# A Conformer stage re-divided between the engines: fewer weight blocks in its opening, the convolution's taps on ScalarE and VectorE alone, side products and last sums moved in TensorE's queue

## The chip, the cores and the metric

The kernel runs on one core of a Trainium2 chip. The metric is the device time of one execution in microseconds (us). Besides the time there is one execution taken with the hardware profiler; its trace lists every instruction of the five engines with start, duration and what ended the idle time before it. Engines are named as the profile does: PE is TensorE's matrix products and PEld its weight loads, DVE is VectorE, ACT is ScalarE, POOL is GpSimd, SP is the queue from which nearly all weight transfers are issued.

## What is computed

Two layers for 256 positions of width 2048. Layer 0 mixes tokens with a Conformer convolution module, layer 1 with a Mamba-2 mixer; each is followed by a squared-ReLU MLP. Shifts, scales and gates of every sub-layer come from a vector `c` by the product with `w_mod`. The change lies in layer 0's mixer:

```python
def conformer_conv(u, w_pw1, b_pw1, w_dw, b_dw, ln_g, ln_b, w_pw2, b_pw2):
    v = u @ w_pw1 + b_pw1                  # 2048 -> 4096
    a, gt = jnp.split(v, 2, axis=-1)
    v = a * jax.nn.sigmoid(gt)             # "GLU"
    v = causal_dwconv(v, w_dw, b_dw)       # 31 taps, per channel
    v = jax.nn.silu(layernorm(v, ln_g, ln_b))
    return v @ w_pw2 + b_pw2

mod = (sc @ w_mod[i] + b_mod[i])[:, None, :]         # sc = silu(c), 6 * 2048 values a layer
sh1, sc1, g1, sh2, sc2, g2 = jnp.split(mod, 6, axis=-1)
h = h + g1 * mix
h = h + g2 * sq_relu_mlp(rmsnorm(h) * (1 + sc2) + sh2, w1, w2)
```

## The kernel before

Activations lie with channels on partitions: 16 channel tiles of 128 channels by 256 positions. Weights come as tiles of 128x2048 f32, 1 MB each, through one SP queue that keeps the order of the program (`stream`). The buffers `w32` (three) hold weight tiles; `wm` (two) and `hid` (four) hold tiles of `w_mod`.

**The opening.** `native(list(range(FIRST)), glu)` works on the first FIRST blocks of `pw1` at once. A block is 512 of the 4096 output columns, that is two channel tiles with their gates. For each of four groups g of the inner dimension `vectors` first makes the modulated input `u[g]` from eight `w_mod` tiles (VectorE's `gemv`, line 255), then each block multiplies its weight tile with it on TensorE (line 583, 16 products of 128x128 by 128x256 a tile). The fourth group goes in halves, each after four of its eight `w_mod` tiles. With FIRST = 4 the fourth block has banks of the pool `ms` and its weight tiles lie in `hid` buffers.

**The convolution stage.** `glu` gates two channel tiles of a block (line 507 on ScalarE, line 508 on VectorE) into one of twelve padded buffers `vpad`. `conv(ct)` then makes 31 taps for a channel tile: 20 products on ScalarE (line 518, 128x256 each, four side by side in a tile), of which two sums of four-wide tiles run on GpSimd (lines 527 and 529) and one on VectorE (528); the other 11 taps are multiply-adds on VectorE (532); lines 534, 535 and 537 fold the four columns. Line 544 takes off the mean of the first tile (`st["m0"]`, from the product of line 541), line 547 squares for the variance. Between three convs each, one more block of `pw1` runs on TensorE.

**The moments.** Sums over channels are taken on TensorE: `moments(g)` adds four tiles and their squares into one `ms` bank (line 558). After the fourth call ScalarE copies the bank (625), TensorE spreads it over the partitions (627), and VectorE and ScalarE make mean and variance (629 to 637), normalise (643 to 648), apply SiLU (649) and split each value for the next product (414 and 415).

**Side products.** Other `w_mod` vectors are made meanwhile, one tile for each `pump`. Those in PE_GROUPS (24 tiles) run on TensorE: line 244 adds four tiles into a row of sums in an `ms` bank, ScalarE copies it (249), four small products turn it into columns (251), ScalarE copies these (253). All others run on VectorE (255, 128x2048 each). The number of tiles is set by RATE_PW1 (in the blocks of the convolution stage), BETWEEN (after the last conv), RATE_PW2 (in `pw2`) and RATE_OPEN (in the opening of the MLP); `need` makes at once what a stage can't start without.

**Order.** A scheduler fixes the order of instructions on each engine ahead of the run; `high_priority` lets a part go first, `issue_after(x)` holds a part behind instruction x. At run time every engine takes its instructions in this order.

The times below carry the line numbers of this text of the kernel:

## Time and profile before

| | us |
|---|---|
| three runs | 2697.23, 2691.67, 2695.97 (median 2695.97) |
| the profiled execution, its own time | 2696.91 |
| span of its instructions | 2695.1 |
| opening, first product to the first gate | 43.0 to 145.7 |
| convolution stage, first gate to the end of the last square | 145.7 to 371.9 |
| last sums and normalisation, to the first products of `pw2` | 371.9 to 402.8 |
| `pw2`, to its last product | 402.8 to 502.4 |
| opening of the MLP, as far as the fourth group's first product | 502.4 to 571.5 |
| the rest (MLP, Mamba, second MLP) | 571.5 to 2695.1 |

A row of the timeline reads: start, duration of the merged piece, engine, line, operation, written tile <- read tiles, shapes, xcount, and in brackets the idle time of the engine just before with what ended it. A product of f32 operands leaves two records in the trace, so x32 is 16 products. A row of the windows gives, for a stretch of time, the busy time of each engine with its count, then TensorE's granted clock (1.00 is full), the busy share of the DMA engines and what they moved. A row of groups ends in busy time, mean ns of one | idle time before them with its releasers. Instructions overlap a little, so the time of one in a row of equals is read from start to start.

### The profile page before, as it was taken

How to read it: one execution, taken by the hardware profiler on the slowest of the kernel's cores; microseconds unless marked ns; L12 is line 12 of the kernel's file. 1: busy time of each engine (PE TensorE's matmuls, PEld its weight loads, DVE VectorE, ACT ScalarE, POOL GpSimd, SP SyncE). 2: the span in 40 equal slices, each digit the busy share in tenths (PEclk: the TensorE clock that was granted, in tenths of full speed). 3: DMA queues.
4: the chain of work that ended last, by engine and by line, in shares of the span. 5: the costliest groups of instructions: out<-in, count | busy, mean ns of one | idle time of the engine just before them, and what ended most of it. 6: DMA issues, size and time to landing. Idle time of an engine off the chain costs nothing.

```text
span 2695.1 us, 37026 instructions
## 1 busy us (share of the span) xinstructions
PE 2540.8 (94%) x14561; PEld 2194.8 (81%) x14561; DVE 2021.8 (75%) x2679; ACT 1345.7 (50%) x2112; POOL 202.4 (8%) x210
## 2 busy tenths in 40 slices
PE   5977759989999999999999999999998999999998
PEld 3865529988888888888888888888897888888886
DVE  6489857898888888888878777888866555565565
ACT  2067554444443443445868666754444344443443
POOL 1033310000000000000100000000000101101000
PEclk9988869999999999999999999999999999999999
DMA  9944458888888888885655555578756555555553
GB/s 385 386 158 146 158 212 318 318 330 320 323 314 324 323 317 327 310 328 176 232 177 184 173 179 190 199 277 316 294 188 218 187 188 189 191 185 200 188 187 141
DMA packets 92593, 657.43 MB, mean 244 GB/s; under 512 B 10465, under 2 KB 10465, under 8 KB 14465
## 3 DMA queue, kind: packets, MB, share of 16 engines
q1 hardware_dynamic: 88274, 640.73, 64.9%
q0 software_dynamic: 3136, 10.59, 1.2%
q10 hardware_dynamic: 1008, 3.75, 0.4%
q8 instruction: 114, 1.87, 0.3%
q14 instruction: 61, 0.50, 0.1%
HBM read 652.83 MB, written 2.20 MB: 243 GB/s over the span
## 4 chain that ended last, share of the span: by engine, by line
PE 86%; DVE 9%; DMA 2%; ACT 1%; issue 1%; SPq 0%; POOL 0%; ACTq 0%; DVEq 0%
PE mm L312 66%; PE mm L364 4%; PE mm L363 4%; PE mm L362 4%; DVE taps L532 4%; PE mm L583 3%; DMA hid<-wmT 1%; DVE taps L534 1%; DVE wl L305 1%; DVE taps L528 1%; PE ms L1031 1%; PE ms L583 1%; DVE wm L255 1%; DMA wm<-wmT 0%; PE ms L244 0%
## 5 line engine op out<-in xcount | busy, mean ns | idle before, releaser
L312 PE MATMUL mm<-u,wh 128*128 128x512 f32 (+1 forms) x4544 | 1372.7, 365 | 13.6 <-ACT wh L304 6.5
L304 ACT CAST wh<-w 128x1024 fp32r<-128x1024 f32 x768 | 807.0, 1051 | 996.3 <-PE mm L312 766.0
L305 DVE TENSOR_TENSOR wl<-w,wh 128x1024 fp32r<-128x1024 f32 x768 | 941.2, 1229 | 455.9 <-ACT wh L304 453.1
L312 PE MATMUL mm<-u,wl 128*128 128x256 f32 x3840 | 1079.2, 283 | 0.7 <-DVE wl L305 0.6
L312 PEld LDWEIGHTS mm<-u,wh 128*128 128x128 f32 x4544 | 814.0, 191 | 157.2 <-ACT wh L304 7.6
L312 PEld LDWEIGHTS mm<-u,wl 128*128 128x128 f32 x3840 | 730.7, 191 | 8.8 <-DVE wl L305 4.7
L312 PE MATMUL mm<-hid,wh 128*128 128x512 f32 (+1 forms) x1344 | 448.3, 384 | 2.5 <-DVE acc L703 2.5
L312 PE MATMUL mm<-hid,wl 128*128 128x256 f32 x1280 | 358.1, 280 | 0.0
L255 DVE SCALAR_TENSOR_TENSOR wm<-wm,scb 128x2048 f32<-128x2048 f32 x133 | 303.9, 2285 | 6.6 <-DMA wm<-wmT 6.3
L312 PEld LDWEIGHTS mm<-hid,wh 128*128 128x128 f32 x1344 | 248.3, 188 | 54.5 <-DVE acc L703 2.8
L312 PEld LDWEIGHTS mm<-hid,wl 128*128 128x128 f32 x1280 | 242.5, 189 | 0.4 <-issue 0.2
L583 PE MATMUL mm<-u,w 128*128 128x256 f32 x896 | 207.6, 393 | 3.5 <-ACT u L500 3.5
L583 PEld LDWEIGHTS mm<-u,w 128*128 128x128 f32 x896 | 176.0, 198 | 38.2 <-issue 8.8
L364 PE MATMUL mm<-wh,hid 128*128 128x512 f32 x512 | 200.0, 391 | 0.0
L362 PE MATMUL mm<-wh,hid 128*128 128x512 f32 x512 | 199.9, 390 | 0.0
L363 PE MATMUL mm<-wl,hid 128*128 128x512 f32 x512 | 199.5, 390 | 0.0
L266 POOL TENSOR_TENSOR mod<-mod,par 128x4 f32<-128x4 f32 (+1 forms) x50 | 38.3, 765 | 1235.3 <-DVE wm L255 1075.6
L532 DVE SCALAR_TENSOR_TENSOR taps<-u,par,taps 128x256 f32<-128x256 f32 x176 | 117.9, 735 | 0.5
L255 DVE SCALAR_TENSOR_TENSOR hid<-hid,scb 128x2048 f32<-128x2048 f32 x35 | 80.0, 2288 | 45.0 <-DMA hid<-wmT 33.9
L364 PEld LDWEIGHTS mm<-wh,hid 128*128 128x128 f32 x512 | 96.1, 188 | 19.7
L362 PEld LDWEIGHTS mm<-wh,hid 128*128 128x128 f32 x512 | 96.2, 188 | 19.6
L363 PEld LDWEIGHTS mm<-wl,hid 128*128 128x128 f32 x512 | 96.1, 188 | 19.6
(211 smaller groups left out, 1766.2 us busy)
## 6 DMA issues: line engine op xcount, KB each, us to landing
w<-w SPq DMA_DIRECT2D x256, 1024.0 KB, 4.9
wm<-wmT SPq DMA_DIRECT2D x145, 1024.0 KB, 7.0
w<-win SPq DMA_DIRECT2D x80, 1024.0 KB, 4.9
hid<-wmT SPq DMA_DIRECT2D x47, 1024.0 KB, 8.4
w<-pw SPq DMA_DIRECT2D x44, 1024.0 KB, 5.1
w<-wout SPq DMA_DIRECT2D x32, 1024.0 KB, 6.7
acc<-ac_d POOLq DMA_DIRECT2D x16, 512.0 KB, 7.2
hid<-pw SPq DMA_DIRECT2D x4, 1024.0 KB, 7.2
```

The source lines that it names most:

```text
L255: nc.vector.scalar_tensor_tensor(out=w, in0=w, scalar=1.0, in1=self.scb, op0=ALU.mult, op1=ALU.mult, accum_out=m[:, i:i + 1])
L266: nc.gpsimd.tensor_tensor(out=m, in0=m, in1=self.col("b_mod", (layer * 6 + seg) * NT + 4 * kg + i0, n), op=ALU.add)
L304: nc.scalar.copy(out=wh, in_=w[:, s, :])
L305: nc.vector.tensor_tensor(out=wl, in0=w[:, s, :], in1=wh.bitcast(F32), op=ALU.subtract)
L312: mm = lambda out, lhsT, rhs, **kw: self.nc.tensor.matmul(out, lhsT=lhsT, rhs=rhs, skip_group_check=True, **kw)
L362: mm(banks[q], lhsT=hi, rhs=wh[:, k, :], start=g == 0 and t == 0, stop=False)
L363: mm(banks[q], lhsT=hi, rhs=wl[:, k, :], start=False, stop=False)
L364: mm(banks[q], lhsT=lo, rhs=wh[:, k, :], start=False, stop=g == 3 and t == 3)
L528: nc.vector.tensor_add(wide, wide, products(four("wl"), 12))
L532: nc.vector.scalar_tensor_tensor(out=o, in0=vp[:, k:k + T], scalar=self.col("w_dw", ct * TAPS + k), in1=o, op0=ALU.mult, op1=ALU.add)
L534: nc.vector.tensor_add(wide, wide, aside)
L583: nc.tensor.matmul(o, lhsT=w[:, t, j * P:(j + 1) * P], rhs=u[g][:, t, :], start=g == 0 and t == 0 and j < 2, stop=g == 3 and t == 3, skip_ ...
```

## The change

- **Three blocks open**: FIRST is 3, all in `w32` buffers and in `mm` banks; the fourth block runs as the first one of the convolution stage, five in all, behind conv 0.
- **Taps**: ScalarE makes 24 products, VectorE adds them in five four-wide sums and makes the other 7 taps. GpSimd makes none.
- **`close`** splits off from `conv` what needs the first tile's mean; for tile 0 it is called from a hook inside the block that follows.
- **Side products**: the row of sums lies in an `mm` bank. Its turning into columns is a method of its own, `columns`, called when the next row of sums has been copied. It and the moments are held behind the last product issued (`self.pe`). RATE_PW1 is 12 tiles over five blocks, BETWEEN is 8 ahead of the last moments and 4 behind the normalisation's instructions; `w_mod` tiles keep going round `wm` and two `hid` buffers.
- **Last moments**: `moments` serves tiles 0 to 11; its bank is copied and spread before the last convs. The sums of tiles 12 to 15 are added by products with `ones` straight into the bank that holds the spread sums.
- The square-root table is loaded behind the last gate, and the subtraction of the mean for the first group moves into the loop over its tiles.

```diff
-RATE_PW1 = spread(10, 16)
-BETWEEN = 10
+RATE_PW1 = spread(12, 20)
+BETWEEN = 8, 4
...
-FIRST = 4
+FIRST = 3
 OPEN = 3
-ACT_TAPS = 20
+ACT_TAPS = 24
...
             if i == 0:
-                self.row_sums = self.bank(self.ms, "ms")
+                self.row_sums = self.bank(self.mm, "mm")
...
             if i == 3:
                 row = self.t("t2", [P, 512], bufs=3)
                 nc.scalar.copy(out=row, in_=self.row_sums)
...
+                self.rows_left.append((row, m, layer, seg, g))
+                if len(self.rows_left) > 1:
+                    self.columns()
+            return
...
+    def columns(self):
+        nc = self.nc
+        row, m, layer, seg, g = self.rows_left.pop(0)
+        ps = self.bank(self.mm, "mm")
+        with self.tc.issue_after(self.pe):
+            for j in range(4):
+                nc.tensor.matmul(ps[:, j:j + 1], lhsT=row[:, j * P:(j + 1) * P], rhs=self.sel[:, :1],
+                                 start=j == 0, stop=True, skip_group_check=True)
+        nc.scalar.copy(out=m, in_=ps[:, :4])
+        self.mod_done(layer, seg, g)
...
             wide = products(four("wh"), 0)
-            pair = self.b("hid", [P, 8, T])
-            aside = products(pair[:, :4, :], 4)
-            nc.gpsimd.tensor_tensor(out=aside, in0=aside, in1=products(pair[:, 4:, :], 8), op=ALU.add)
-            nc.vector.tensor_add(wide, wide, products(four("wl"), 12))
-            nc.gpsimd.tensor_tensor(out=aside, in0=aside, in1=products(four("wl"), 16), op=ALU.add)
+            for k in range(4, ACT_TAPS, 4):
+                nc.vector.tensor_add(wide, wide, products(four("wl"), k))
             for k in range(ACT_TAPS, TAPS):
...
-            nc.vector.tensor_add(wide, wide, aside)
...
         native(list(range(FIRST)), glu)
-        self.rings = ("wm", "hid")
...
-        ct = 0
-        for b in range(FIRST, 8):
+        y = conv(0)
+        native([FIRST], glu, pump=pump, hook=lambda: close(0, y))
+        ct = 1
+        for b in range(FIRST + 1, 8):
             for _ in range(3):
-                conv(ct)
+                close(ct, conv(ct))
                 ct += 1
...
+            if b >= 6:
+                moments(b - 6)
             native([b], glu, pump=pump)
+        with self.tc.issue_after(st["gate"]):
+            nc.scalar.activation(out=self.t("rcol", [P, 2])[:, :1], in_=self.eps, func=AF.Sqrt)
+        self.pump(BETWEEN[0])
+        moments(2)
+        rows = self.t("t2", [P, 2 * T], bufs=3)
+        nc.scalar.copy(out=rows, in_=st["sums"])
+        ps = self.bank(self.mm, "mm")
+        with self.tc.issue_after(self.pe):
+            nc.tensor.matmul(ps, lhsT=self.sel, rhs=rows, start=True, stop=False, skip_group_check=True)
         while ct < NT:
-            conv(ct)
+            close(ct, conv(ct))
             ct += 1
-        moments(2)
-        self.pump(BETWEEN)
...
-            moments(3)
-            rows = self.t("t2", [P, 2 * T], bufs=3)
-            nc.scalar.copy(out=rows, in_=st["sums"])
-            ps = self.bank(self.mm, "mm")
-            nc.tensor.matmul(ps, lhsT=self.sel, rhs=rows, start=True, stop=True)
+            for i in range(12, NT):
+                for e in range(2):
+                    self.pe = nc.tensor.matmul(ps[:, e * T:(e + 1) * T], lhsT=self.ones, rhs=st["sq"][i][e], start=False,
+                                               stop=i == NT - 1, skip_group_check=True).ins
...
+        with self.tc.issue_after(self.pe):
+            self.pump(BETWEEN[1])
```

TensorE at the last moments, before: `lo` and `nrm` are the squares of the last tiles, `scol` marks a side product (its tile of `w_mod` in `hid` or `wm`), `bT` with `t` the turning into columns, and the last row is the spreading of the sums (line 627).

```order
L558 MATMUL ms_1254<-nrm_1821,ones 32x256
L244 MATMUL ms_1856<-wm_1861,scol 32x512 x4
L244 MATMUL ms_1856<-hid_1867,scol 32x512 x4
L244 MATMUL ms_1856<-wm_1873,scol 32x512 x4
L251 MATMUL ms_1856<-bT_114,t_259_1879 128x1 x4
L244 MATMUL ms_1890<-hid_1887,scol 32x512 x4
L244 MATMUL ms_1890<-wm_1895,scol 32x512 x4
L244 MATMUL ms_1890<-hid_1901,scol 32x512 x4
L244 MATMUL ms_1890<-wm_1907,scol 32x512 x4
L251 MATMUL ms_1890<-bT_114,t_265_1913 128x1 x4
L627 MATMUL mm_1933<-t_266_1931,bT_114 128x512
```

The same place in the changed kernel, where the spreading is line 634 and the direct sums are line 643:

```order
L571 MATMUL ms_1378<-sq_1582,ones 32x256
L634 MATMUL mm_1828<-t_281_1826,bT_114 128x512
L643 MATMUL mm_1828<-acc_203,ones 128x256
L643 MATMUL mm_1828<-lo_1629,ones 128x256
L643 MATMUL mm_1828<-acc_203,ones 128x256
L643 MATMUL mm_1828<-nrm_1875,ones 128x256
L643 MATMUL mm_1828<-acc_203,ones 128x256
L643 MATMUL mm_1828<-lo_1922,ones 128x256
L643 MATMUL mm_1828<-acc_203,ones 128x256
L643 MATMUL mm_1828<-nrm_1969,ones 128x256
L245 MATMUL mm_2057<-hid_2054,scol 32x512 x4
```

No side product stands between the last square and the sums any more: eight tiles stand ahead of the moments of tiles 8 to 11, four behind the last sum.

TensorE inside a block of the convolution stage, before (here `u_186` and `u_187` are the third and fourth group of the modulated input, `w` a weight tile):

```order
L244 MATMUL ms_857<-wm_1104,scol 32x512 x4
L583 MATMUL mm_1058<-u_186,w_168_1102 128x256 x2
L251 MATMUL ms_857<-bT_114,t_170_1110 128x1 x4
L583 MATMUL mm_1058<-u_186,w_168_1102 128x256 x6
L583 MATMUL mm_1059<-u_186,w_168_1102 128x256 x8
L244 MATMUL ms_1139<-hid_1136,scol 32x512 x4
L583 MATMUL mm_1058<-u_187,w_171_1134 128x256 x8
```

and in the changed kernel, in block 7:

```order
L245 MATMUL mm_1445<-hid_1685,scol 32x512 x4
L591 MATMUL mm_1639<-u_186,w_258_1683 128x256 x8
L591 MATMUL mm_1640<-u_186,w_258_1683 128x256 x8
L245 MATMUL mm_1445<-hid_1709,scol 32x512 x4
L269 MATMUL mm_1717<-bT_114,t_224_1415 128x1 x4
L591 MATMUL mm_1639<-u_187,w_260_1707 128x256 x8
L591 MATMUL mm_1640<-u_187,w_260_1707 128x256 x8
```

Before, the columns of a row of sums (`ms_857`) stood two products behind the last tile of the same row. Now they stand behind the last tile of the next row: `t_224` was copied from the bank `mm_1144`, whose last tile stands in block 6.

VectorE in the convolution stage, before, one channel tile (`hid` is GpSimd's sum):

```order
L528 TENSOR_TENSOR taps_926<-taps_926,taps_941 128x1024
L532 SCALAR_TENSOR_TENSOR taps_926<-u_185,par,taps_926 128x256 x11
L534 TENSOR_TENSOR taps_926<-taps_926,hid_931 128x1024
L535 TENSOR_TENSOR taps_926<-taps_926 128x512
L537 TENSOR_TENSOR taps_926<-taps_926 128x256
L544 TENSOR_TENSOR acc_200<-taps_926,ssum_739 128x256
```

and now, where the end of one tile (`taps_1090`) stands between the sums of the next (`taps_1237`):

```order
L539 TENSOR_TENSOR taps_1237<-taps_1237,taps_1242 128x1024
L544 TENSOR_TENSOR taps_1090<-taps_1090 128x512
L539 TENSOR_TENSOR taps_1237<-taps_1237,taps_1248 128x1024
L546 TENSOR_TENSOR taps_1090<-taps_1090 128x256
L539 TENSOR_TENSOR taps_1237<-taps_1237,taps_1254 128x1024
L558 TENSOR_TENSOR acc_201<-taps_1090,ssum_708 128x256
L539 TENSOR_TENSOR taps_1237<-taps_1237,taps_1260 128x1024
L539 TENSOR_TENSOR taps_1237<-taps_1237,taps_1266 128x1024
L542 SCALAR_TENSOR_TENSOR taps_1237<-u_186,par,taps_1237 128x256 x7
```

A channel tile has five wide sums in place of two, 7 taps in place of 11, and no operand from GpSimd.

More of the change, by code (lines that the diff above doesn't have):

```diff
@@ L164, in __init__ @@
         self.mod = {}
+        self.rows_left = []
         self.prologue()
@@ L634, in conformer @@
             nc.scalar.activation(out=var, in_=var, func=AF.Sqrt, bias=self.eps)
-            for t in range(4):
-                nc.vector.tensor_sub(dd[0][:, t, :], dd[0][:, t, :], mean)
             nc.vector.reciprocal(var, var)
```

66 lines of the change are left out of this document (32 added, 34 removed).

## The prediction

> **What bounds the kernel now.** The windows by stage come first, then the timeline of each engine where a stage waits.
>
> ```profile
> 43.00:145.70 102.70, 100.91 (x457) 88.15 (x458) 60.69 (x62) 7.94 (x16) 3.16 (x16) 1.00 0.86 351
> 145.70:371.90 226.20, 158.13 (x756) 121.61 (x759) 194.72 (x272) 149.48 (x371) 81.45 (x38) 0.83 0.42 154
> 371.90:402.80 30.90, 19.11 (x96) 5.83 (x88) 11.41 (x19) 13.60 (x25) 1.00 (x5) 0.67 0.75 306
> 402.80:502.40 99.60, 99.60 (x790) 94.80 (x791) 79.61 (x97) 45.96 (x70) 3.43 (x8) 0.97 0.87 330
> 502.40:571.50 69.10, 59.40 (x465) 58.35 (x463) 62.77 (x81) 28.95 (x40) 1.91 (x5) 0.91 0.80 314
> 571.50:2695.10 2123.60, 2093.35 (x11985) 1820.85 (x11985) 1587.76 (x2115) 1085.84 (x1564) 105.23 (x102) 0.99 0.66 238
> ```
>
> The last row, four fifths of the time, is TensorE's (2093 of 2124 us) and the change leaves it alone. In the opening TensorE is nearly full and the DMA at 351 GB/s. The convolution stage is VectorE's: 195 of 226 us, TensorE 158. In the last sums nothing is full. `pw2` is TensorE's again; in the opening of the MLP TensorE stands still for 9.7 us.
>
> Why VectorE needs 14 us for a channel tile is seen in its taps, once beside GpSimd's sums and once without:
>
> ```profile
> 349.28 8.50 DVE L532 SCALAR_TENSOR_TENSOR taps<-u,par,taps 128x256 f32<-128x256 f32 x11
> 309.33 4.45 DVE L532 SCALAR_TENSOR_TENSOR taps<-u,par,taps 128x256 f32<-128x256 f32 x11
> 357.88 1.23 DVE L534 TENSOR_TENSOR taps<-taps,hid 128x1024 f32<-128x1024 f32 x1
> 359.14 0.69 DVE L535 TENSOR_TENSOR taps<-taps 128x512 f32<-128x512 f32 x1
> 360.33 0.42 DVE L544 TENSOR_TENSOR acc<-taps,ssum 128x256 f32<-128x256 f32 x1
> L529 POOL TENSOR_TENSOR hid<-hid,taps 128x1024 f32<-128x1024 f32 x16 | 40.2, 2513 | 35.4 <-ACT taps L518 20.7 <-DVE taps L532 14.4
> ```
>
> Eleven taps cost 4.45 us alone (0.40 each) and 8.50 beside GpSimd, whose sum lasts 2.5 us: VectorE stands still meanwhile. TensorE waits too, for copies that stand far down in ScalarE's order:
>
> ```profile
> 171.39 1.19 PE L541 MATMUL mm<-taps,ones 128*128 128x256 f32 x2 [13.62 <-DVE taps L537]
> 237.78 1.84 PE L251 MATMUL ms<-bT,t 128*128 128x1 f32 x8 [16.02 <-ACT t L249]
> 265.60 14.08 PE L583 MATMUL mm<-u,w 128*128 128x256 f32 x64
> 279.61 1.06 PE L244 MATMUL ms<-hid,scol 128*32 128x512 f32 x8
> 309.35 1.86 PE L251 MATMUL ms<-bT,t 128*128 128x1 f32 x8 [18.23 <-ACT t L249]
> ```
>
> **The opening: -9.5 us.**
>
> ```profile
> 72.67 20.88 PE L583 MATMUL mm<-u,w 128*128 128x256 f32 x96
> 52.14 14.14 SPq L289 DMA_DIRECT2D w<-pw  x3
> 50.00:60.00 10.00, 10.00 (x48) 8.81 (x47) 9.33 (x9) 0.00 (x0) 0.00 (x0) 1.00 1.01 420
> 115.00:125.00 10.00, 10.00 (x48) 8.81 (x47) 3.09 (x4) 0.91 (x2) 0.31 (x2) 1.00 0.62 209
> 131.51 2.29 DVE L255 SCALAR_TENSOR_TENSOR hid<-hid,scb 128x2048 f32<-128x2048 f32 x1 [13.27 <-DMA hid<-wmT]
> 143.69 10.63 PE L583 MATMUL mm<-u,w 128*128 128x256 f32 x48 [1.79 <-ACT u L500]
> 145.72 0.47 ACT L507 ACTIVATE a<-mm,par 128x256 f32<-128x256 f32 x1 [0.39 <-PE mm L583]
> ```
>
> Three blocks need 20.9 us of TensorE a group, so four groups no longer fill it. What remains is the DMA: the last half waits for `w_mod` tiles (13.27 us). At 420 GB/s a tile takes 1.049 MB / 420 = 2.5 us. The first three weight tiles of group 1 are issued up to 66.3 (52.14 + 14.14) as TensorE frees the buffers, with three blocks as with four. From there 26 tiles land before; with about 2 us latency and the 5 us lost at 115 to 125 (209 of 420 GB/s) this gives 66.3 + 2 + 65 + 5 = 138.3. Now 23 tiles: 57.5, and of the loss I keep 3, since the third weight buffer still waits for TensorE: 128.8, 9.5 earlier. Bounds: 7.5 with the whole loss, 12.5 with none. [...]
>
> **The convolution stage: -33.5 us.** Each engine's share, from the first gate on.
>
> VectorE, a tile: five sums at 1.23, seven taps at 0.40, 0.69 + 2 x 0.42, and the gating 0.48: 11.0, for 16 tiles 176 us. No GpSimd stands in its way.
>
> ```profile
> 345.64 4.98 ACT L518 ACTIVATE taps<-u,par 128x256 f32<-128x256 f32 x12
> 367.77 1.71 ACT L669 ACTIVATE h<-h,gb 128x256 f32<-128x256 f32 x4 [0.90 <-POOL gb L666]
> 371.47 0.42 ACT L547 ACTIVATE nrm<-acc 128x256 f32<-128x256 f32 x1 [2.00 <-DVE acc L544]
> 393.15 1.28 ACT L634 ACT_TABLE_LOAD   x1
> 365.61 1.05 PE L251 MATMUL ms<-bT,t 128*128 128x1 f32 x8 [0.69 <-ACT t L249]
> L583 PE MATMUL mm<-u,w 128*128 128x256 f32 x552 | 130.5, 398 | 0.0
> ```
>
> ScalarE: 384 products at 0.41 (4.98 / 12) are 157 us; 16 gates (0.46), 16 squares and 16 updates of h (0.42 each), copies and a table load about 25: 182 us.
>
> TensorE (of the rows above the last two are its own): it now has five blocks here. A weight tile is 7.04 us (14.08 for two), a block 28.2. From the first gate it still works 8.5 us on the opening (143.69 + three blocks x 3.5 - 145.7). Then up to the gate of tile 14 come four blocks (112.8), 3.5 weight tiles (24.6), twelve side tiles at 1.0 (279.61 to 280.60), two groups of columns at 1.05, two moments at 1.0 and the first mean 0.5: 162.5 us. In the trace of before its waits in this stage end on ScalarE's copy; in the new order the copies that it needs stand well ahead: the first turning (line 269) comes a whole block after its copy. ScalarE reaches the gate of tile 14 after 336 products, at 138 us and 18 for 14 gates, 14 squares, 8 updates and the copies, 156, and must wait for TensorE. That is the new bound, and a close one.
>
> From there the last two tiles: 48 products 19.7, gate and gating 0.9, table load 1.28, three copies and two squares 2.3, then VectorE's last sum, seven taps and folds 1.23 + 2.8 + 1.5 and a square 0.42: 30 us. The stage lasts 192.5 where it lasted 226.2. Bounds: TensorE's products at the mean of 0.47 that they had in this stage with its restarts (130.5 us for 276, the last row) instead of 0.44 add 9; ScalarE alone, 182 plus 6 for the drain, takes off 4.5, and products at 0.40 three more.
>
> A new wait is ScalarE's copy of the moments (line 631), with tile 15's products queued behind it. Its sums stand behind eight side tiles and two turnings, done some 12 us after block 7, that is at about 178; ScalarE gets there after tile 14's products, two copies and a table load, at about 179. Nothing, then; if one of the eight comes late, what it lacks is added in full. SP's queue can run ahead to those tiles, since all weight tiles of the stage stand before them.
>
> The other moved steps cost nothing that I can see. The mean of tile 0 is copied by ScalarE behind 51 products, at 23 us; its product on TensorE stands behind two weight tiles and a side tile, at 8.5 + 14.1 + 1.0 = 23.6. ScalarE may lose 1 or 2 us, within the 6 that it has in hand; without them they would count. The DMA has 20 weight tiles and some 18 of `w_mod` to bring, 38 x 2.5 = 95 us in a stage of 190. The moments of tiles 0 to 7 stand behind squares that are 30 us old. The square-root table (1.28) moves from the last sums into the tail, where I have counted it; the subtraction that moves into the loop is the same work.
>
> **The last sums: -17 us.**
>
> ```profile
> 371.51 0.63 PE L558 MATMUL ms<-nrm,ones 128*32 128x256 f32 x1
> 382.41 1.06 PE L244 MATMUL ms<-hid,scol 128*32 128x512 f32 x8 [1.43 <-DMA hid<-wmT]
> 389.27 2.06 PE L627 MATMUL mm<-t,bT 128*128 128x512 f32 x2
> 391.36 0.42 DVE L629 TENSOR_SCALAR a<-mm 128x256 f32<-128x256 f32 x1 [19.92 <-PE mm L627]
> 402.79 1.86 PE L312 MATMUL mm<-u,wh 128*128 128x256 f32 x7 [1.61 <-DVE u L415]
> ```
>
> From the last square (371.9) to VectorE's first step (391.36) lie 19.5 us, in which TensorE makes side products, some waiting for their tile, and only then spreads the sums. Two direct products remain, 2 x 0.63 in that clock, and VectorE may still be in a weight split (1.2): 2.5 us. The 11.4 us of normalisation stay; the four side tiles behind the last sum (4 x 1.0) and a turning fit into them. TensorE has little to do ahead of `pw2` then. It starts there at a low clock already before (0.67 in the window), so I add nothing. [...]
>
> **`pw2` and the opening of the MLP: -3 and -6 us.**
>
> ```profile
> 426.32 1.07 PE L244 MATMUL ms<-wm,scol 128*32 128x512 f32 x8
> L255 DVE SCALAR_TENSOR_TENSOR wm<-wm,scb x133: 2280/2284/2294, 16.1 to 2032.3; 128x2048 f32<-128x2048 f32 x133
> 561.12 2.29 DVE L255 SCALAR_TENSOR_TENSOR wm<-wm,scb 128x2048 f32<-128x2048 f32 x1
> 568.15 0.91 ACT L417 ACTIVATE u<-nrm,mod 128x256 fp32r<-128x256 f32 x2 [11.92 <-POOL mod L266]
> ```
>
> All 24 side tiles of TensorE are now done by the last sums, where 20 were. `pw2` loses three to four at 1.0, as TensorE's time. VectorE gets four more at 2.29, 9 us, against 20 that it has free there (99.6 - 79.6); without that cover each would cost 2.3. In the MLP's opening before, 45 of 48 tiles are there for the fourth group, so `need` makes three on the spot (the rows at 561 to 568) and TensorE waits. Now 49 are; 3 x 2.29 = 6.9 goes from VectorE, 6 from TensorE's 9.7 us standstill (bounds 3 and 7).
>
> **The sum.** -9.5 - 33.5 - 17 - 3 - 6 = -69, on the profiled execution's own 2696.9 (0.9 above the median of the three runs): 2628 us. The terms' bounds together reach from -50 (7.5 + 24.5 + 15 + 0 + 3) to -85 (12.5 + 41 + 18 + 6 + 7): 2647 to 2612. Those of the last sums are a full weight split more, and none; those of `pw2` are its VectorE work in the way, and the low clock at its start gone.
>
> **Rivals.** For one of them a row on the time from issue to landing, from the list of DMA issues:
>
> ```profile
> hid<-wmT SPq DMA_DIRECT2D x47, 1024.0 KB, 8.4
> ```
>
> - *The hand-off sets the pace* (0.17). ScalarE, VectorE and TensorE are within a tenth of each other, and ScalarE has three buffers ahead of VectorE. If a tile takes 12.5 us for waits between them, where the sums say 11 to 11.4, the stage is 16 x 12.5 + 11 for start and drain = 211: 2646. For it: before, VectorE needed 14 where its own work was 8 to 9. Against: there GpSimd explains the rest.
> - *ScalarE's bound and no loss in the opening* (0.12). TensorE keeps ahead, products at 0.40: the stage is 180 to 185, the opening gives 12: 2615.
> - *Slower: side products hold TensorE* (0.04). Twelve side tiles stand inside the blocks, each ahead of weight products; a late tile holds the block, the gate and ScalarE. The change is lost if each waits 5.8 us (69 / 12); with the 8.4 us of the row above, 101 us come on: 2729. Against: each tile is issued at least one weight tile (7 us) ahead of its use, and waits like the 1.43 at 382.41 come where many such tiles follow each other.
> - *TensorE's restarts* (part of the forecast's range): +9, 2637.
>
> The forecast has 0.67, its own range 2614 to 2641. For 8 times in 10 I take 2608 to 2648, which holds the first two rivals. Faster by over 0.2% (what a measurement of this kernel can tell): 0.95; within 0.2%: 0.01; slower: 0.04.
>
> **What would show it.** Right: first gate at 136 or so; line 542's median and mean equal; last square near 329; line 646 within 3 us of it; first products of `pw2` near 341; no forced tiles in the MLP's opening, fourth group's first product near 501. ScalarE's one long wait should be the gate of tile 14, on TensorE. Wrong: ScalarE waiting for VectorE's sums in every tile (the first rival), or TensorE's line 245 waiting for `hid` and `wm` inside the blocks (the third). A first gate later than 140 would put the opening's bound elsewhere than in the DMA.

## The result, and the profile after

| | before | after |
|---|---|---|
| median of four runs, us | 2696.6 (2691.67 to 2697.99) | 2629.12 (2627.93 to 2632.18) |
| profiled execution, us (span) | 2696.9 (2695.1) | 2629.66 (2627.8) |

The ratio is 0.9755, 95% interval 0.9738 to 0.9772: 67.5 us faster, where 69 were forecast. Of all runs below one execution, of d_order_split, was slow (6446.82 us, cause unknown); the median of that run is the same without it. First the windows of the kernel after by stage (opening, convolution stage, last sums with normalisation, `pw2`, opening of the MLP, rest), to be laid beside the six rows of before; the columns are TensorE, weight load, VectorE, ScalarE, GpSimd, clock, DMA share, GB/s.

```profile
43.00:143.40 100.40, 81.37 (x345) 69.91 (x346) 60.17 (x62) 7.78 (x16) 3.13 (x16) 0.89 0.78 317
143.40:339.70 196.30, 185.16 (x937) 142.56 (x937) 167.92 (x257) 180.93 (x447) 8.14 (x8) 0.96 0.69 262
339.70:352.00 12.30, 8.27 (x48) 3.57 (x48) 12.27 (x21) 7.45 (x15) 1.09 (x3) 0.78 0.64 249
352.00:446.70 94.70, 93.03 (x757) 92.83 (x757) 85.82 (x101) 43.51 (x66) 5.53 (x9) 0.97 0.83 325
446.70:516.00 69.30, 65.73 (x527) 64.97 (x526) 64.22 (x85) 33.99 (x49) 4.49 (x4) 0.95 0.80 303
516.00:2627.80 2111.80, 2084.06 (x11936) 1809.31 (x11934) 1578.13 (x2104) 1082.30 (x1558) 107.39 (x102) 0.99 0.67 238
```

In the stage TensorE went from 158 of 226 us to 185 of 196, and ScalarE from 149 to 181. The opening is the row that doesn't fit the forecast: the DMA moves 317 GB/s instead of 351, and TensorE has 19 us of standstill, 8.7 of them ahead of the third group and 10.3 ahead of the last half group. Its rows in the timeline of the kernel after (start, length, engine, line; in brackets the idle time before and what ended it):

```profile
94.96 34.31 PE L591 MATMUL mm<-u,w 128*128 128x256 f32 x144 [8.71 <-ACT u L513]
105.12 14.14 SPq L301 DMA_DIRECT2D w<-pw  x3
119.32 0.42 SPq L301 DMA_DIRECT2D hid<-wmT  x1
119.85 0.36 SPq L301 DMA_DIRECT2D wm<-wmT  x1
120.70 0.81 SPq L301 DMA_DIRECT2D hid<-wmT  x2
126.60 2.29 DVE L255 SCALAR_TENSOR_TENSOR hid<-hid,scb 128x2048 f32<-128x2048 f32 x1 [13.70 <-DMA hid<-wmT]
139.58 5.91 PE L591 MATMUL mm<-u,w 128*128 128x256 f32 x13 [10.32 <-ACT u L513]
143.40 0.47 ACT L520 ACTIVATE a<-mm,par 128x256 f32<-128x256 f32 x1 [2.17 <-PE mm L591]
```

SP's queue stands for 14 us at three weight tiles that wait for TensorE to free their buffers, and the last four tiles of `w_mod` stand behind them. The end of the convolution stage and the last sums, same columns:

```profile
306.36 0.47 ACT L520 ACTIVATE a<-mm,par 128x256 f32<-128x256 f32 x1 [1.11 <-PE mm L591]
319.69 1.94 PE L245 MATMUL mm<-hid,scol 128*32 128x512 f32 x8 [2.66 <-DMA hid<-wmT]
321.56 1.87 PE L269 MATMUL mm<-bT,t 128*128 128x1 f32 x8
323.46 0.16 ACT L271 COPY mod<-mm 128x4 f32<-128x4 f32 x1 [1.18 <-PE mm L269]
325.36 0.59 ACT L631 COPY t<-ms 128x512 f32<-128x512 f32 x1 [1.32 <-PE ms L571]
339.27 0.42 ACT L561 ACTIVATE nrm<-acc 128x256 f32<-128x256 f32 x1 [0.76 <-DVE acc L558]
341.42 0.42 DVE L646 TENSOR_SCALAR a<-mm 128x256 f32<-128x256 f32 x1
```

The first row is the gate of tile 14, the last VectorE's first step of the normalisation. Between them a side tile waits for its transfer, and ScalarE waits twice behind it, with tile 15's products in its queue.

Two more views: the taps on VectorE, and the ReLU of the MLPs, whose first start is a mark below (shortest/median/longest in ns, first and last start), for after and, in the last row, before.

```profile
L542 DVE SCALAR_TENSOR_TENSOR taps<-u,par,taps x112: 475/480/486, 159.1 to 337.1; 128x256 f32<-128x256 f32 x112
L751 ACT ACTIVATE a<-mm x24: 373/384/387, 513.9 to 1964.0; 128x256 f32<-128x256 f32 x24
```

```profile
L730 ACT ACTIVATE a<-mm x24: 371/384/387, 577.7 to 2024.2; 128x256 f32<-128x256 f32 x24
```

Where the 67.3 us of span came from, with the forecast beside it (each figure rounded by itself):

| term | before | after | gain | forecast |
|---|---|---|---|---|
| start to first gate | 145.7 | 143.4 | 2.3 | 9.5 |
| first gate to end of last square | 226.2 | 196.3 | 29.9 | 33.5 |
| to VectorE's first step | 19.5 | 1.7 | 17.7 | 17 |
| to the first ReLU (normalisation, `pw2`, MLP's opening) | 186.3 | 172.5 | 13.8 | 9 |
| first ReLU to the end | 2117.4 | 2113.9 | 3.5 | 0 |

### The profile page after: what moved, and what is told of

Same layout as the page of the kernel before. It is cut to its first block, busy times and chain, and to the rows that moved or that the text cites. A ratio compares the mean times of both kernels' runs of the same rounds, so it can differ in the third digit from the quotient of the medians.

```text
span 2627.8 us, 37071 instructions
## 1 busy us (share of the span) xinstructions
PE 2528.1 (96%) x14561; PEld 2188.6 (83%) x14561; DVE 1993.5 (76%) x2663; ACT 1370.0 (52%) x2176; POOL 136.0 (5%) x178
## 4 chain that ended last, share of the span: by engine, by line
PE 91%; DVE 3%; DMA 3%; ACT 1%; issue 1%; POOL 0%; ACTq 0%; SPq 0%; DVEq 0%
PE mm L325 66%; PE mm L591 8%; PE mm L377 4%; PE mm L376 4%; PE mm L375 4%; DMA hid<-wmT 2%; DVE wl L317 1%; PE mm L245 1%; PE ms L1052 0%; DVE wm L255 0%; PE ms L446 0%; ACT acc L665 0%; PE ms L460 0%; DMA h<-xT 0%; PE ms L1021 0%
## 5 line engine op out<-in xcount | busy, mean ns | idle before, releaser
L255 DVE SCALAR_TENSOR_TENSOR wm<-wm,scb 128x2048 f32<-128x2048 f32 x129 | 294.7, 2285 | 2.1 <-DMA wm<-wmT 2.0
L591 PE MATMUL mm<-u,w 128*128 128x256 f32 x1024 | 233.0, 389 | 20.7 <-ACT u L513 20.7
L591 PEld LDWEIGHTS mm<-u,w 128*128 128x128 f32 x1024 | 198.6, 195 | 58.4 <-ACT u L513 21.8
L531 ACT ACTIVATE taps<-u,par 128x256 f32<-128x256 f32 x384 | 158.2, 502 | 0.6 <-DVE u L522 0.6
L255 DVE SCALAR_TENSOR_TENSOR hid<-hid,scb 128x2048 f32<-128x2048 f32 x39 | 89.1, 2287 | 40.6 <-DMA hid<-wmT 29.7
```

Source lines behind the costliest of these rows:

```text
L255: nc.vector.scalar_tensor_tensor(out=w, in0=w, scalar=1.0, in1=self.scb, op0=ALU.mult, op1=ALU.mult, accum_out=m[:, i:i + 1])
L531: nc.scalar.activation(out=p4[:, q, :], in_=vp[:, k + q:k + q + T], func=AF.Identity, scale=self.col("w_dw", ct * TAPS + k + q), bias=self ...
L591: self.pe = nc.tensor.matmul(o, lhsT=w[:, t, j * P:(j + 1) * P], rhs=u[g][:, t, :], start=g == 0 and t == 0 and j < 2, stop=g == 3 and t == 3,
```

## The experiments

Twelve more kernels ran. All are read on the same marks, in us of the profiled execution: the starts of the first gate, of the last square (it lasts 0.4 us), of VectorE's first step and of the first ReLU. The time is the median, the ratio that to the runs of before taken beside it.

| run | first gate | last square | VectorE's first step | first ReLU | span | time | ratio, 95% interval |
|---|---|---|---|---|---|---|---|
| before | 145.7 | 371.5 | 391.4 | 577.7 | 2695.1 | 2696.6 | 1 |
| after | 143.4 | 339.3 | 341.4 | 513.9 | 2627.8 | 2629.12 | 0.9755 (0.9738 to 0.9772) |
| b_first3 | 143.7 | 400.8 | 420.6 | 606.9 | 2727.7 | 2727.51 | 1.011 (1.0095 to 1.0125) |
| b_first3b | 143.7 | 391.1 | 410.9 | 595.1 | 2716.4 | 2719.07 | 1.0082 (1.0068 to 1.0095) |
| b_conv24 | 145.5 | 326.0 | 340.2 | 526.4 | 2647.1 | 2647.51 | 0.9814 (0.9798 to 0.9831) |
| a_gpsimd | 143.4 | 380.1 | 382.3 | 556.9 | 2670.6 | 2671.9 | 0.9903 (0.9888 to 0.9917) |
| a_oldsums | 143.0 | 333.9 | 338.6 | 515.7 | 2629.5 | 2631.15 | 0.9756 (0.9741 to 0.977) |
| a_side20 | 143.5 | 330.8 | 333.0 | 518.5 | 2639.3 | 2638.12 | 0.978 (0.9763 to 0.9796) |
| a_order | 136.4 | 329.5 | 331.7 | 504.6 | 2618.9 | 2617.73 | 0.9707 (0.9693 to 0.9722) |
| a_warm | 141.8 | 334.0 | 336.1 | 510.9 | 2624.0 | 2623.91 | 0.9727 (0.9707 to 0.9747) |
| c_first4 | 146.6 | 335.6 | 337.3 | 509.6 | 2626.5 | 2624.39 | 0.9726 (0.971 to 0.9741) |
| d_order_split | 135.3 | 327.9 | 330.1 | 503.0 | 2616.8 | 2618.66 | 0.9717 (0.9703 to 0.973) |
| d_order_split_t20 | 136.5 | 330.1 | 332.6 | 505.2 | 2618.2 | 2620.46 | 0.9722 (0.9706 to 0.9739) |
| d_first4_hook_t20 | 146.6 | 333.1 | 334.8 | 506.7 | 2620.5 | 2622.89 | 0.9733 (0.9719 to 0.9746) |

**Why the opening gave 2.3 us and not 9.5.** The theory from the trace was SP's queue; the rival was the prediction's own, the rate of the DMA. The kernel after, with the transfers of the fourth group's second half issued ahead of the weight tiles:

```diff
+                if opening:
+                    for t0, t1 in halves:
+                        vectors(g, t0, t1)
                 for n, (t0, t1) in enumerate(halves):
-                    if opening:
-                        vectors(g, t0, t1)
```

> The kernel after with one move: in the fourth group of the opening the eight transfers of w_mod that make the second half are issued ahead of the three weight tiles, which wait on SP's queue for TensorE to free their buffers. Theory: this queue, and not the rate of the DMA, sets the first gate; the last w_mod tiles land about 10 us earlier, TensorE's two standstills of about 10 us shrink, first gate at 133 to 137 instead of 143.4: 6 to 10 us faster than the kernel after, 2619 to 2623. Rival, the prediction's: the rate of the DMA bounds the opening, the order of the transfers changes nothing in their sum: first gate 141 to 143, at most 2 us faster. Second rival: the weight tiles now come late instead, and the first half waits for them: no gain, 2629.

The rows of its timeline that answer to those above, and its opening and stage among the windows:

```profile
95.64 22.45 PE L591 MATMUL mm<-u,w 128*128 128x256 f32 x96 [8.73 <-ACT u L513]
104.68 2.82 SPq L301 DMA_DIRECT2D hid<-wmT  x2
107.60 30.86 SPq L301 DMA_DIRECT2D w<-pw  x4
122.36 17.90 PE L591 MATMUL mm<-u,w 128*128 128x256 f32 x74 [4.27 <-DMA w<-pw]
136.41 0.47 ACT L520 ACTIVATE a<-mm,par 128x256 f32<-128x256 f32 x1 [9.72 <-PE mm L591]
```

```profile
43.00:136.40 93.40, 80.34 (x345) 69.20 (x346) 60.15 (x62) 8.05 (x17) 5.14 (x16) 0.95 0.83 341
136.40:329.90 193.50, 182.68 (x937) 141.21 (x936) 167.90 (x257) 180.81 (x447) 7.92 (x8) 0.98 0.69 262
80.00:90.00 10.00, 6.91 (x33) 5.73 (x31) 9.20 (x9) 0.00 (x0) 0.00 (x0) 1.00 1.02 424
```

The same tiles and the same bytes, in another order, bring the first gate 7.0 us forward, to 136.4. The theory holds: it was the order in the queue, not the rate of the DMA, that delayed the last part of the opening. The second rival shows in part, for TensorE now waits 4.3 us for a weight tile. The other standstill, 8.7 us ahead of the third group, is the same in both kernels. The third row, from the time just before it, has the DMA at 424 GB/s and a share of 1.02 (the highest rate in any 5 us of the traces of before and after, counted in steps of 5 us, is 433 GB/s), so there its rate does bind (with VectorE, busy for 9.2 of these 10 us on the same tiles, close behind). The stage also became 2.8 us shorter, and the time is 11.4 us below that of the kernel after.

The other part of the shortfall was looked for in TensorE's clock:

```diff
+WARM = 10
...
+                            for i in range(WARM):
+                                self.pe = nc.tensor.matmul(idle, lhsT=self.ones, rhs=self.scb[:, :512], start=i == 0,
+                                                           stop=i == WARM - 1, skip_group_check=True).ins
...
```

> The kernel after with ten products of a constant tile (128x512, results thrown away) on TensorE between the two halves of the opening's fourth group, where it stood still for 10.3 us. Theory: the last half group runs at the full clock, 2.0 us to the first gate instead of 3.8: first gate at 141.5 instead of 143.4, and nothing else moves: 2627 to 2628. Rival 1: the half clock does not come from the standstill, the first gate stays at 143.4, 2629. Rival 2: the ten products last longer than the gap and push the half group back: first gate at 145 or later, 2631.

The windows around the last half group, of the kernel after and then of this one, and this one's rows in the timeline (the half group, the first gate, and the side tile that comes late):

```profile
130.00:140.00 10.00, 0.42 (x1) 0.42 (x2) 7.67 (x8) 0.96 (x3) 0.77 (x4) 0.58 0.30 125
140.00:145.00 5.00, 5.00 (x13) 3.87 (x13) 0.48 (x1) 1.70 (x2) 0.00 (x0) 0.50 0.00 0
```

```profile
140.00:145.00 5.00, 5.00 (x24) 4.36 (x24) 0.97 (x2) 3.34 (x7) 0.00 (x0) 1.00 0.09 13
```

```profile
139.76 6.53 PE L592 MATMUL mm<-u,w 128*128 128x256 f32 x29 [1.72 <-ACT u L514]
141.79 0.47 ACT L521 ACTIVATE a<-mm,par 128x256 f32<-128x256 f32 x1 [0.38 <-PE mm L592]
315.45 1.06 PE L246 MATMUL mm<-hid,scol 128*32 128x512 f32 x8 [1.07 <-DMA hid<-wmT]
```

The half group starts at 139.8 as before, but the granted clock is 1.00 instead of 0.50, and the first gate comes 2.0 us later instead of 3.8. So the half clock (0.50 behind 10.3 us of standstill in the kernel after) does come from the standstill; how short a standstill would do is not shown. The gate of tile 15 moves by more, from 310.3 to 307.6, and VectorE's first step from 341.4 to 336.1: three times the 1.8 us expected. So 2.7 us are there by the last gate, for the half clock went on behind the first gate (in the kernel after it was 0.50 from 143.4 to 145.0, 0.82 in the next us and 1.00 from 146 on). The other 2.6 come in the tail, where the side tile waits 1.07 us for its transfer instead of 2.66 and ScalarE no longer waits for the copies behind it; why that transfer was earlier isn't shown, and there is one trace of each kernel. The intervals of the two ratios overlap; the clock and the first gate are shown by the trace, a gain in the whole time is not shown clear of noise.

**What each part is worth in the stage.** Three blocks in the opening alone, in the kernel before, in two versions. In the first the convolution of tile 14 stood ahead of its gate and read old data, which also held that gate up; only its first gate (143.7) is used here.

```diff
-RATE_PW1 = spread(10, 16)
+RATE_PW1 = spread(10, 20)
...
-FIRST = 4
+FIRST = 3
...
-            for _ in range(3):
+            for _ in range(1 if b == FIRST else 3):
```

The last pair of lines stands in the second version alone.

> The kernel before with one part of the change: three blocks in the opening instead of four (side tiles of the stage spread over 20 weight tiles instead of 16). Theory from the two traces: the opening is held by the order of the transfers behind TensorE's weight buffers, so the first gate comes only 2 to 3 us earlier (143 instead of 145.7); VectorE and GpSimd still need 14 us for a channel tile, so the stage keeps its 226 us and takes the 28 us block of TensorE in its standstills: 2.5 us faster, about 2694. Rival 1, the DMA term of the prediction: first gate near 136, 9.5 us faster, about 2687. Rival 2: TensorE's waits for ScalarE's copies (13 to 18 us each) now lie on the path, the stage becomes longer than 230 us: slower than before by 5 to 15 us.

> The kernel before with three blocks in the opening, as in the first such run, but with one convolution ahead of the fourth block instead of three, so that tile 14's convolution again stands behind its gate (in the first such run it stood ahead of it, read old data, and held that gate up). Theory: first gate 143.4, 2 us earlier; VectorE and GpSimd still set the pace, so TensorE's 28 us more fill its standstills: within 4 us of before, 2693 to 2699. Rival: TensorE's waits for ScalarE's copies (13 to 20 us each) leave it no room, and the stage grows by 10 us or more: over 2704.

The first gate of the first version, 143.7, lies where its theory has it and not at the 136 of its first rival. Of the second version the rival holds: alone, this edit makes the kernel slower, by 0.8% or 22 us. The first gate comes 2.0 us earlier, and the stage takes 247.8 us instead of 226.2. TensorE's waits for ScalarE's copies are no longer than before (before has 36.3 us in five), but with a fifth block behind them the gates come later: VectorE waits for gates 36.5 us in the stage, where it waited 19.4. The list of waits of this run:

```profile
PE ms L251 <- ACT t L249: 32.5, 5, 15.7
```

The columns are us in total, times, longest. That these waits make the gates late is read from the trace; no run removes them alone. The convolution alone, in the kernel before:

```diff
-ACT_TAPS = 20
+ACT_TAPS = 24
...
-            aside = products(pair[:, :4, :], 4)
-            nc.gpsimd.tensor_tensor(out=aside, ...)
...
+            for k in range(4, ACT_TAPS, 4):
+                nc.vector.tensor_add(wide, wide, products(four("wl"), k))
...
```

> The kernel before with one part of the change: 24 taps' products on ScalarE, all sums on VectorE, none on GpSimd; four blocks in the opening and TensorE's old order stay. Theory: the taps on VectorE take 0.40 us each throughout and VectorE needs 11 us for a tile; ScalarE's 182 us become the bound of the stage, 226 to about 200; the last sums get shorter by some 8 us as well, since the sums no longer hold buffers that the side tiles need: 30 to 36 us faster, about 2662. Rival: TensorE's old order, which waits 13 to 18 us three times for copies that stand far down in ScalarE's queue, sets the pace once VectorE is out of the way: the stage stays above 215 us and the gain is under 15 us.

```profile
145.50:326.40 180.90, 155.12 (x787) 118.37 (x785) 166.22 (x256) 174.49 (x436) 2.73 (x6) 0.92 0.52 195
```

```profile
316.48 1.06 PE L554 MATMUL ms<-acc,ones 128*32 128x256 f32 x2 [9.02 <-DVE acc L540]
328.77 1.06 PE L244 MATMUL ms<-wm,scol 128*32 128x512 f32 x8 [0.17 <-DMA wm<-wmT]
331.22 1.06 PE L244 MATMUL ms<-hid,scol 128*32 128x512 f32 x8 [1.38 <-DMA hid<-wmT]
333.70 1.93 PE L244 MATMUL ms<-wm,scol 128*32 128x512 f32 x8 [1.42 <-DMA wm<-wmT]
340.16 0.43 DVE L625 TENSOR_SCALAR a<-mm 128x256 f32<-128x256 f32 x1 [16.69 <-PE mm L623]
```

This part brings 50 us, three quarters of the whole, and more than either theory had expected. The stage is 180.9 us, 15 shorter than in the kernel after, with ScalarE busy for 174.5 of it. The last sums still take 13.8 us (326.4 to 340.2), for the side products stand on TensorE behind moments that wait for VectorE (the row at 316.48) and some then wait for their tile. The opposite undoing, the kernel after with the convolution of before:

> The kernel after with the convolution of before: 20 taps on ScalarE, the sums of 12 of them on GpSimd, 11 taps on VectorE. Theory: the taps on VectorE are again of two kinds, 0.40 and about 0.77 us, VectorE needs 14 us for a tile and 16 tiles 224 us; the stage grows from 196 to about 225, the side tiles come late again for want of buffers: 30 to 38 us slower, about 2663. Rival: TensorE's 163 us to the gate of tile 14 stay the bound, VectorE only lengthens the tail by two or three tiles' difference: 6 to 10 us slower, about 2637.

```profile
L545 DVE SCALAR_TENSOR_TENSOR taps<-u,par,taps x176: 469/474/2595, 156.1 to 376.7; 128x256 f32<-128x256 f32 x176
```

42.8 us slower, where the theory had 30 to 38; it holds, with a stage of 237.1 us instead of 225. The longest tap takes 2595 ns, about as long as a GpSimd sum, where without GpSimd it takes 486. The trace of before has both cases: of the eleven taps from 361.9 on one took 2575 ns, beside a GpSimd sum of 2.47 us from 362.55; of the eleven from 309.3 on, with no sum beside them, none took over 485 ns.

If five blocks make TensorE the bound, four should leave ScalarE as the bound. The kernel after with four blocks in the opening:

```diff
-RATE_PW1 = spread(12, 20)
+RATE_PW1 = spread(12, 16)
...
-FIRST = 3
+FIRST = 4
...
+            banks = [[self.bank(self.mm, "mm") if i < 3 else self.bank(self.ms, "ms") for _ in range(2)]
...
-            for _ in range(3):
+            for _ in range(4):
                 close(ct, conv(ct))
```

> The kernel after with its opening put back to four blocks (the fourth in a buffer of hid and the two banks of ms, as before); four convolutions instead of three stand ahead of each of the last three blocks, so that 13 tiles precede the last weight tiles as in the kernel after. Theory: the block that the change took out of the opening is what made TensorE the bound of the stage; without it ScalarE's own 181 us set it (as in the run with the convolution alone): first gate 145.5, last square near 327, VectorE's first step near 329.5 instead of 341.4: 10 to 12 us faster than the kernel after, about 2618. Rival: 181 us came from TensorE's old order or its fewer side tiles; with 24 side tiles done by the last sums the stage is 194 again and the opening 2 us longer: about 2631.

```profile
146.60:336.00 189.40, 163.83 (x826) 120.86 (x824) 169.33 (x259) 181.69 (x448) 3.08 (x8) 0.91 0.65 250
```

VectorE's first step comes 4.1 us earlier than in the kernel after, not 10 to 12. The stage is 189.4 us: shorter than with three blocks (196.3), longer than the 180.9 of the convolution alone. The theory is right in its direction. Most of the 8.5 us between the two is work: ScalarE is busy for 181.7 us here and for 174.5 there. By its groups of instructions the 7.2 us more are three weight casts of `pw2` (3.1), four more updates of h (1.5), the table load with its step (1.5) and copies (1.2). The time is 4.7 us below that of the kernel after, with intervals that overlap.

**The last sums and what follows.** The old form of the sums in the kernel after. Of the twelve side tiles eight stand ahead of the last sums here and four behind, as in the kernel after, other than the expectation says.

```diff
-        self.pump(BETWEEN[0])
-        moments(2)
-        rows = self.t("t2", [P, 2 * T], bufs=3)
-        nc.scalar.copy(out=rows, in_=st["sums"])
...
         while ct < NT:
             close(ct, conv(ct))
             ct += 1
-
+        moments(2)
+        self.pump(BETWEEN[0])
...
-            for i in range(12, NT):
-                for e in range(2):
...
+            moments(3)
+            rows = self.t("t2", [P, 2 * T], bufs=3)
+            nc.scalar.copy(out=rows, in_=st["sums"])
+            ps = self.bank(self.mm, "mm")
+            self.pe = nc.tensor.matmul(ps, lhsT=self.sel, rhs=rows, start=True, stop=True).ins
...
```

> The kernel after with its last sums put back: the sums of tiles 12 to 15 go into the rows as those of the others, all 12 side tiles of this place stand ahead of them on TensorE, then one copy and the spreading product. Theory: the 17 us came mostly from the side tiles being there in time (their buffers are no longer held by the sums of the taps), so TensorE has done them before the last square; what comes back is the eight short sums 1.0, a copy 0.6, the spreading product 1 to 2 and the hand-overs: 4 to 6 us slower, about 2634. Rival, the prediction's reason: the order of the sums behind the side products cost the 17 us, and the last sums take 15 to 18 us more: about 2645.

```profile
309.54 1.04 PE L245 MATMUL mm<-wm,scol 128*32 128x512 f32 x8
319.17 1.06 PE L245 MATMUL mm<-hid,scol 128*32 128x512 f32 x8 [1.41 <-DMA hid<-wmT]
333.91 0.42 ACT L561 ACTIVATE nrm<-acc 128x256 f32<-128x256 f32 x1
335.88 0.59 ACT L637 COPY t<-ms 128x512 f32<-128x512 f32 x1 [0.62 <-PE ms L571]
336.52 2.07 PE L639 MATMUL mm<-t,bT 128*128 128x512 f32 x2 [0.68 <-ACT t L637]
338.63 0.42 DVE L641 TENSOR_SCALAR a<-mm 128x256 f32<-128x256 f32 x1
```

From the end of the square to VectorE's first step lie 4.3 us instead of 1.7, so the direct products are worth 2.6 of the 17.7; the other 15 are the side tiles, which now are through before the last square (the first and the last of the eight are the first two rows). The rival falls, with eight tiles ahead and not the twelve that it names. Of these 15 us the convolution alone takes 5.7 (13.8 us in b_conv24 instead of 19.5). The rest came with the new place of the side tiles, eight instead of ten and directly behind block 7; number and place were not taken apart. And the direct form costs what it brings: its copy of the moments stands among tile 15's products, where ScalarE waits for it. Here, without it, the last square comes 190.9 us behind the first gate instead of 195.9. The time is the same within the noise.

The larger gain behind the sums (to the first ReLU) was laid to the count of side tiles done by then, 24 instead of 20:

```diff
-RATE_PW1 = spread(12, 20)
+RATE_PW1 = spread(8, 20)
```

> The kernel after with four side tiles fewer inside the blocks (8 instead of 12), so that 20 of the 24 on TensorE are done before pw2 as in the kernel before, and four stand in pw2. Theory: this supply is where pw2, the opening of the MLP and the rest won their 17 us: the stage itself gets up to 4 us shorter, pw2 4 to 5 longer, the MLP's opening waits again for three to four forced tiles (6 to 8) and a little of the rest comes back: 5 to 12 us slower than the kernel after, 2634 to 2641. Rival: the 17 us come from the new places of the turnings, not from the count: the four tiles only move their 4 us from the stage to pw2, 2629.

```profile
331.20:518.50 187.30, 173.87 (x1351) 164.67 (x1351) 159.95 (x201) 85.76 (x132) 8.59 (x18) 0.91 0.79 305
```

```profile
PE mm L325 <- ACT wh L316: 6.1, 1, 6.1
```

VectorE's first step comes 8.4 us earlier, and from there to the first ReLU it takes 185.5 us instead of 172.5, about what before had (186.3); TensorE's 6.1 us wait for the forced tiles is back. 9 us slower in all: the theory holds. The rest of the kernel grew by 6.9 us. That part goes with the count as well: first ReLU to the end takes 2117.4 to 2121.3 us in the five kernels with 20 tiles done (before, b_first3, b_first3b, b_conv24, a_side20) and 2113.0 to 2116.9 in the nine with 24. By which path the count acts there is not shown.

**Versions that beat both.** To a_order were added a split of the eight side tiles around the moments, and then 20 taps on ScalarE. A third kernel has the split and the 20 taps with four blocks and tile 0 closed one weight tile earlier, but with the transfers of the opening in the order of the kernel after.

```diff
-        self.pump(BETWEEN[0])
+        self.pump(BETWEEN[0] // 2)
         moments(2)
         rows = self.t("t2", [P, 2 * T], bufs=3)
         nc.scalar.copy(out=rows, in_=st["sums"])
+        self.pump(BETWEEN[0] // 2)
```

> The kernel of the run with the transfers issued ahead in the opening (2617.7), and one move more: of the eight side tiles behind block 7 four stand ahead of the moments of tiles 8 to 11 and their copy on ScalarE, four behind them, so that the copy no longer waits for a side tile whose transfer is late. Theory: ScalarE's wait at that copy in the kernel after (1.3 us, and 1.2 at the one before) is on the path and goes: last square 187 to 191 us behind the first gate instead of 193 to 196, 2 to 4 us faster than 2617.7, 2614 to 2616. Rival: the wait only moves to the next copy of a row in the same queue, no change, 2618.

> As the run before it in this list, with 20 taps on ScalarE and 11 on VectorE (none on GpSimd). Theory: the gate of tile 14 stays where TensorE puts it, 163 us behind the first gate, since ScalarE and VectorE both have room; the tail has 8 products less on ScalarE (3.3 us) and on VectorE a sum less and four taps more for the last tile (0.4 us): 2 to 4 us faster than without, 2611 to 2614. Rival: VectorE, at 11.4 us a tile instead of 11.0 and with the weight splits of pw2 to prepare, becomes the bound of the tail: no gain or 2 us lost, 2615 to 2618.

> The kernel after with four blocks in the opening (as in the run of that), its tile 0 closed one weight tile earlier, the side tiles split around the moments as above, and 20 taps on ScalarE, 11 on VectorE. Theory: with TensorE out of the way the stage is set by VectorE (16 tiles at 11.4 us) and ScalarE (182 less 64 products at 0.41, 156): 182 to 186 us from a first gate at 146, last square near 330, and about 2286 less 10.3 from there: 2614 to 2618, 7 to 10 us faster than with four blocks and 24 taps on ScalarE (2624.4). Rival: VectorE has no room for it, the stage stays at 190 and the time at 2624.

The split's theory fails: the last square comes 192.6 us behind the first gate instead of 193.1, and the medians don't tell the two apart. In a_order the waits at the two copies were 1.3 us already, where the theory took the 2.5 of the kernel after. With 20 taps on ScalarE nothing is gained (the last square comes 193.6 us behind the first gate): its rival holds. With four blocks the theory fails too: the stage is 186.9 us, 2.5 less than with 24 taps, though ScalarE is busy for 25 us less (156.7), and the time is 2622.9, not 2614 to 2618. The best median is a_order's, 2617.73: 79 us below before and 11 below after.

## Why the prediction was right, point by point

- **The opening** is the mis-sized term: 2.3 for 9.5. The step that failed is "What remains is the DMA": it counted 23 tiles at 2.5 us from 66.3 on and took the loss to shrink. (The 2 us of latency in it cancel in the difference; the trace of before has a transfer of 64 KB that took 2.1 us from issue to landing.) For the third group it was right (8.7 us of standstill, with the DMA at 420 GB/s and a share of 1.01 from 85 to 95). For the last half group the loss grew instead, since the transfers wait on SP's queue for TensorE. The DMA's rows at 420 GB/s were read as a bound for the whole, though the stretch at 209 GB/s stood beside them. The prediction's own test said it: a first gate later than 140 meant another bound, and it was 143.4. With the order changed the gate came at 136.4, where the forecast had it; that is another kernel, with a wait of 4.3 us that the forecast doesn't have, so it doesn't prove the sum. The half clock behind the standstill (0.50, 1.8 us to the gate) was not forecast; a low clock was weighed for `pw2` alone.
- **The stage**: 29.9 for 33.5. The path through TensorE was right to half a microsecond: the gate of tile 14 came 163.0 us behind the first (162.5 forecast), with TensorE busy all that time, and a_side20, with four side tiles fewer, has its last gate 161.0 us behind the first instead of 166.9. The tail was 33.3 instead of 30. The wait that was named and priced at nothing, ScalarE's copy behind a late side tile, cost some 2.5 us (1.18 and 1.32 in the rows above); in a_warm, where ScalarE doesn't wait there, the tail is 30.7.
- What the forecast did not see: it never set the stage with four blocks beside that with five. With four blocks ScalarE is the busiest engine (174.5 of 180.9 us and 181.7 of 189.4), near the 182 that the forecast dismissed as not the bound. It isn't the only limit there: with 20 taps on it the stage was still 186.9, with VectorE busy for 173.3, and what sets that is open. Taking a block out of the opening is a loss alone (b_first3b), and within the change it cost up to 4.7 us (c_first4). With the transfers reordered three blocks were better than any kernel with four (2617.7 against 2622.9), but four blocks with that order were not run.
- **The last sums**: 17.7 for 17. What took the time before was named rightly, the side products ahead of the spreading. The kernel also ends the stage as forecast, with two direct products behind the last square. But the gain hardly hangs on them: a_oldsums has 15 us of it with the old sums, since the side tiles are done before the last square there too, and the direct sums themselves bring 2.6.
- **`pw2` and the opening of the MLP**: 13.8 for 9, with normalisation 1.1, `pw2` 3.4, the MLP's opening 9.3. The border is the last product of `pw2` on TensorE's timeline, 503.4 and 448.9; the rows of the windows cut 1 and 2 us ahead of it. The mechanism, 24 side tiles done ahead instead of 20, is shown by a_side20; `pw2` was sized well and the MLP's opening low. Another 3.5 us in the rest were not forecast; in the list of waits one of TensorE for ScalarE, in the second layer, is 6.6 us before and 2.0 after, at code that the change doesn't touch. It is 6.4 in a_side20, so it too follows the count of side tiles:

```profile
PE ms L764 <- ACT wm L765: 6.6, 3, 4.5
```

```profile
PE ms L785 <- ACT wm L786: 2.0, 2, 1.5
```

- Of the rivals, the hand-off did not set the pace (TensorE 185 of 196 us), ScalarE's bound did not hold with five blocks, and no side tile inside the blocks held TensorE (busy for all 163.0 us to the gate of tile 14). The total came within 2 us by luck: in the profiled executions 10.8 us too much in the first two terms met 9 too little in the last three.

## What to carry to other kernels

Where a transfer's lane looks full, look at what the issuing queue stands on: here three weight tiles held four others for 14 us, and putting the ones with free buffers first brought the first gate 7.0 us forward, where taking out a quarter of the work had brought 2.3. Before work is moved from one stage into another, write down each engine's count for the stage both with and without it; here the move of one block gave back 7 of the 45 us that the new convolution had won in the stage. A total that comes out right proves no term: check each at its own mark.

## What the hardware showed that was not expected

After a standstill of 10.3 us the last half group ran at a clock of 0.50. With ten products of no use in the gap it ran at 1.00, and the last gate, some 166 us later, came 2.7 us earlier, where 1.8 were expected; VectorE's first step came 5.3 us earlier, of which 2.6 are explained only by a transfer that landed earlier in that trace. GpSimd's sums stretch single VectorE taps to 2595 ns against 486 without them, while the median stays at 474: the mean shows it, not the median (735 ns against 474 in the kernel before, 480 against 480 in the kernel after).
